# Fourier units spread over two stages, and the modulation steps beside them moved, in a diffusion step's mixing layer

## The chip, the cores and the metric

The kernel runs on one core of a Trainium2 chip. It computes one inference step of one layer for 128 context and 256 latent tokens (384 rows, D = 2048). The metric is device time in microseconds of one launch; the median of three runs stands for a kernel.

## The reference

```python
def mixer(h, s0_f, s0_b, n_chunks, lw):
    proj = h @ lw['w_in']
    q, k, v, g, lr_f, lr_b, fo = jnp.split(proj, splits, axis=-1)
    ...
    o = (o * jax.nn.silu(g.astype(jnp.float32))).astype(h.dtype)     # GLA branch
    fg = fo.astype(jnp.float32).reshape(bsz, t, FOURIER_GROUPS, FOURIER_GROUP_DIM)
    f = jnp.fft.fft2(fg, axes=(1, 3), norm='ortho').real             # Fourier branch
    f = f.reshape(bsz, t, FOURIER_WIDTH).astype(h.dtype)
    gates = jax.nn.sigmoid(h @ lw['w_gate'] + lw['b_gate'])
    g_a, g_b = jnp.split(gates, 2, axis=-1)
    merged = g_a * (o @ lw['w_br_gla']) + g_b * (f @ lw['w_br_four'])
    return merged @ lw['w_out'], s_f, s_b

def layer(x, cond, s0_f, s0_b, n_chunks, lw):
    mod = jax.nn.silu(cond) @ lw['w_ada'] + lw['b_ada']
    sh1, sc1, ga1, sh2, sc2, ga2 = [m[:, None, :] for m in jnp.split(mod, N_MOD, axis=-1)]
    h = rmsnorm(x, lw['norm_pre_mix']) * (1.0 + sc1) + sh1
    m, s_f, s_b = mixer(h, s0_f, s0_b, n_chunks, lw)
    x = x + ga1 * rmsnorm(m, lw['norm_post_mix'])
    h = rmsnorm(x, lw['norm_pre_ffn']) * (1.0 + sc2) + sh2
    ff = (jax.nn.silu(h @ lw['w_ffn_gate']) * (h @ lw['w_ffn_up'])) @ lw['w_ffn_down']
    x = x + ga2 * rmsnorm(ff, lw['norm_post_ffn'])
    return x, s_f, s_b
```

## The kernel before

Activations lie transposed, channels on partitions and the 384 tokens along the rows. Every fp32 product is made of three matmuls on parts in the type fp32r: each weight tile `raw` (128 x 1024, 512 KB) is split into `whi`, a rounded copy made by ScalarE (L218), and `wlo`, the rest, made by VectorE (L219). `gemm` (L252) then multiplies hi by hi, hi by lo and lo by hi.

The weight tiles come in one list `srcs`, in the order in which the products use them. `grab` (L239) hands out the oldest split tile and issues the load and the split of the tile three places further on. `raw` has two buffers, `whi` and `wlo` four each. PE, ScalarE, VectorE and GpSimd keep the order of the program; the order of SP's DMA queue is made by the scheduler when the kernel is built. All DMAs of this part stand in SP's queue.

The stages up to the output projection are: modulation and the first projections; gates and GLA scans (`rate` 1.0); the Fourier projections with the DFT of each group beside them (8 double tiles, `rate` 0.7); the **merge stage**, which the change touches; and the output projection (32 tiles, `rate` 0.6). Beside them a generator `ada_rest` (L555) works out the remaining modulation vectors in steps: 16 full steps per half vector (load 512 KB `adaw`, two VectorE operations on 128 x 1024, L564 and L566), then an empty step, one with 16 small matmuls `pr` (L574), and one with two transposes `ptm`, which also begins the next half. `paced` (L266) takes `rate` steps for each call, so a `rate` of 0.25 is one step in four calls. What is left after output unit 12 is done at once.

The merge stage walks through `mix_order` (L155). It has three kinds of units:

- `o`, 8 of them: one 128-channel tile of GLA's output gate, two weight tiles (48 matmuls `pmm`), then `gcol` (L971): three transposes `pt`, SiLU on ScalarE (with its table), `gs` and `o_lo` on VectorE.
- `b`, 16 of them, `four` (L980): one tile of the Fourier branch's projection, one weight tile, and 34 matmuls `pf` (L990 to L993). Its weight tile is folded first: VectorE makes sums and differences of column pairs (`ws`, L199 and L200) and the split is made of these. Behind PE come two copies on ScalarE and, on VectorE, `fd` (L995), four parts of `y` (L999, L1000) and the product with the gate (L1003). `y` is then written to `four_d` in device memory. If the tile that a `b` unit or an `a` unit prepares is itself a folded one, its split is held until the unit's own work on VectorE is issued (`settle`); in an `o` unit it is made at once.
- `a`, 16 of them: one tile of the GLA branch's projection, one weight tile (24 matmuls), then the product with its gate (L1026), the sum with the `y` of the `b` unit of the same number, read back from `four_d` (L1027, L964), and in the next `a` unit its split into `A_hi` and `A_lo`.

An `a` unit needs all eight `o` units and its own `b` unit. Behind each unit of kind `a` or `b`, `gate_of` (L954) loads the gate (and for `a` the `y`) of the unit two places on and applies the sigmoid to the next one. The order before is o0, o1 b0 b1, o2 b2 b3, ..., o7 b12 b13, then a0 b14 a1 b15, then a2 to a15.

Of the kernel before, what the change touches and what calls it, by code (L numbers as in the profile page):

```python
# [22 lines left out]
KT = D // P  # L23
# [73 lines left out]
def tile_step(ctx: ExitStack, tc: tile.TileContext, a, o):  # L97
# [35 lines left out]
    def alloc_A():  # L133
        return tuple(actp.tile([P, KT, T], F32R, tag=f"A_{n}", name=f"A_{n}") for n in ("hi", "lo"))
# [17 lines left out]
    for i in range(16, 24):  # L152
        srcs += two(a["w_in"], i)

    mix_order = [("o", 0)]  # L155
    for i in range(1, 8):
        mix_order += [("o", i), ("b", 2 * i - 2), ("b", 2 * i - 1)]
    mix_order += [("a", 0), ("b", 14), ("a", 1), ("b", 15)] + [("a", i) for i in range(2, KT)]
    folded = set()
    for b, i in mix_order:  # L160
        if b == "o":
# [66 lines left out]
    def settle():  # L228
        if half_done:
            half_done.pop()()  # L230
# [8 lines left out]
    def grab(hold=False):  # L239
        w = take()  # L240
        push(hold=hold)
        return w

    def step(side):
        if side is not None:
            next(side, None)

    def gemm(dst, w, x, kts, n=P, n0=0, k0=0, first=True, last=True):

        for k in range(kts):  # L250
            for j, (wi, xi) in enumerate(((0, 0), (0, 1), (1, 0))):
                PE.matmul(  # L252
                    dst, w[wi][:, k * n + n0 : k * n + n0 + P], x[xi][:, k0 + k, :],
                    start=first and k == 0 and j == 0, stop=last and k == kts - 1 and j == 2,
                )

    def proj(pool, x, dst, side=None):

        p = pool.tile([P, T], F32, tag="mm", name="pmm")
        for g in range(2):  # L260
            gemm(p, grab(), x, 8, k0=8 * g, first=g == 0, last=g == 1)
            if g:
                dst(p)
            step(side)
# [12 lines left out]
    def split_act(hi, lo, src):  # L277
        ACT.copy(hi, src)
        DVE.tensor_sub(lo, src, hi.bitcast(F32))
# [323 lines left out]
    rate = [1.0]  # L603
# [238 lines left out]
    with ExitStack() as s:  # L842
# [64 lines left out]
        def nyq_weights():  # L907

            n = D // 2
            for h in range(2):  # L910
                wr = pc.tile([P, n], F32, tag="ws", name="wr")
                POOL.memset(wr, 0.0)
                for g in range(4):
                    src = a["w_br_four"][8 * h : 8 * h + 8, 32 * g : 32 * g + 1, (2 * g + 1) * P : (2 * g + 2) * P]
                    SP.dma_start(
                        wr[g : g + 65 : 32, :].rearrange("p (i c) -> p i c", c=P),
                        src.rearrange("i p c -> p i c").to_broadcast([3, 8, P]),
                    )
                    if g % 2:
                        yield  # L920
                w = wn[:, n * h : n * h + n]
                ACT.copy(w, wr)
                DVE.tensor_sub(w[32:64], wr[32:64], w[32:64].bitcast(F32))
                yield
# [8 lines left out]

        sd = side()
        nw = nyq_weights()
        rate[0] = 0.7
        for i in range(8):
            def fo(p, i=i):
                if i % 2 == 0:
# [14 lines left out]
        def gate_of():  # L954

            u = next(gorder, None)
            if u is not None:
                b, i = u
                g = pc.tile([P, T], F32, tag="gate", name="gate", bufs=4)
                SP.dma_start(g, gates_d[i + (16 if b == "b" else 0)])  # L960
                y = None
                if b == "a":
                    y = pc.tile([P, T], F32, tag="yb", name="yb", bufs=4)
                    SP.dma_start(y, four_d[i])  # L964
                gates[u] = g, y
                raw_gates.append(g)
            if raw_gates and (u is None or len(raw_gates) > 1):
                g = raw_gates.pop(0)
                ACT.activation(g, g, AF.Sigmoid)

        def gcol(p, i):  # L971
            pt = pss.tile([P, T], F32, tag="side", name="pt")
            for t in range(3):
                PE.transpose(pt[:, t * P : (t + 1) * P], on(t, i // 2)[:, i % 2, :], ident)
            g = pc.tile([P, T], F32, tag="gs", name="gs")
            ACT.activation(g, p, AF.Silu)
            DVE.scalar_tensor_tensor(g, g, gnorm[:, i : i + 1], pt, op0=ALU.mult, op1=ALU.mult)
            split_act(oT[0][:, i, :], oT[1][:, i, :], g)

        def four(i):  # L980

            w = grab(hold=True)
            d = pc.tile([P, 2, HT], F32, tag="fd", name="fd")
            y = pc.tile([P, T], F32, tag="yb", name="y", bufs=4)
            for m, x in enumerate((eT, dT)):

                pf = (pss if m else psm).tile([P, 512], F32, tag="side" if m else "mm", name="pf")
                for k in range(4):
                    c = slice(512 * m + k * P, 512 * m + (k + 1) * P)
                    PE.matmul(pf[:, 0 : 2 * HT], w[0][:, c], x[k], start=k == 0, stop=False)  # L990
                    PE.matmul(pf[:, 0:HT], w[1][:, c], x[k][:, 0:HT], start=False, stop=m == 1 and k == 3)  # L991
                if m == 0:
                    PE.matmul(pf[:, 0:HT], wn[0:96, i * P : (i + 1) * P], pnr[0:96], start=False, stop=True)  # L993
                ACT.copy(d[:, m], pf[:, HT : 2 * HT])
                DVE.tensor_add(d[:, m], d[:, m], pf[:, 0:HT])  # L995
            g, _ = gates.pop(("b", i))
            for lo, n, base in ((0, TC, 0), (TC, TL, HC)):
                h = n // 2
                DVE.tensor_add(y[:, lo : lo + h], d[:, 0, base : base + h], d[:, 1, base : base + h])  # L999
                DVE.tensor_sub(  # L1000
                    y[:, lo + h : lo + n], d[:, 0, base + h : base : -1], d[:, 1, base + h : base : -1],
                )
            DVE.tensor_mul(y, y, g)  # L1003
            SP.dma_start(four_d[i], y)
            settle()

        rate[0] = 0.25
        mT, late = None, []
        for b, i in mix_order:
            if b == "o":  # L1010
                if i == 1:
                    gate_of()
                proj(psm, hT, lambda p: gcol(p, i), sd)
                if i == 1:
                    gate_of()
                continue
            if b == "b":
                four(i)
            else:
                if mT is None:  # L1020
                    mT = alloc_A()
                    rate[0] = 0.15
                p = psm.tile([P, T], F32, tag="mm", name="pmm")
                gemm(p, grab(hold=True), oT, 8)
                g, y = gates.pop((b, i))
                DVE.tensor_mul(g, g, p)  # L1026
                DVE.tensor_add(y, y, g)  # L1027
                settle()
                if late:
                    split_act(*late.pop())  # L1030
                late.append((mT[0][:, i, :], mT[1][:, i, :], y))
                step(sd)
            gate_of()
# [6 lines left out]
    with ExitStack() as s:  # L1040
# [42 lines left out]
            ACT.activation(sq2, mg32(i), AF.Square)  # L1083
            return sq0, pr, sq2

        rate[0] = 0.6
        spare_h = {-4: ((pe, "hid_hi", 1), (pe, "hid_lo", 1)), -2: ((pe, "S0", 1), (pe, "S1", 1))}
        spare_w = ((adap, "adaw", 2), (adap, "adaw", 2))
        raw2 = None
# [382 lines left out]
        for u in range(HEAD):  # L1472
            kind, c, j = ffn_order[u]
# [316 lines left out]
```

## Time and profile before

| | |
|---|---|
| timed runs, median (lowest, highest) | 1972.66 us (1972.44, 1972.72) |
| profiled execution, first to last instruction (span) | 1970.6 us |
| the rest of a run around such a span | 2.1 us, by the median |
| TensorE matmuls busy | 1949.7 us |
| VectorE busy | 1629.0 us |
| merge stage on PE, o2 to a15 | 603.6 to 767.1 us of the span |

The profiled execution has no time of its own beside its span, so the span is compared with the median. In the profile PE is the matmul part of TensorE, PEld its weight loads, DVE VectorE, ACT ScalarE, POOL GpSimd and SPq SyncE's DMA queue. A row of the timeline gives start and duration in us, engine, line, operation, what is written from what, and in brackets how long the engine had stood idle and what ended that. A matmul's end is modelled and neighbours overlap.

### The profile page before, as it was taken

The numbers are of one execution on the slowest core, as the hardware profiler recorded it, in microseconds if no ns is written. First come the engines' busy times: TensorE is split into PE (matmuls) and PEld (weight loads), VectorE is DVE, ScalarE is ACT, GpSimd is POOL, SyncE is SP. The second block draws the span as 40 slices with busy tenths as digits, with TensorE's granted clock in tenths as the row PEclk, the third lists the DMA queues.
The fourth block names the chain that finished last, engine by engine and source line by source line (L and its number), as shares of the span: only waits on it lengthen the run. The fifth ranks groups of instructions, "written<-read, shape, count | busy, mean of one in ns | idle before, by whom it ended". The sixth has DMA issues, their size and how long they took to land.

```text
span 1970.6 us, 27516 instructions
## 1 busy us (share of the span) xinstructions
PE 1949.7 (99%) x10576; PEld 1727.3 (88%) x10576; DVE 1629.0 (83%) x2075; ACT 908.9 (46%) x1281; POOL 32.2 (2%) x44
## 2 busy tenths in 40 slices
PE   8999999999999999999999999999999999999998
PEld 6779999999999999999988888888888888888886
DVE  5569788878767878877789998999899989887875
ACT  4233554544345655446454444354444444444444
POOL 0000000000000000004000000000000000000001
PEclk9999999999999999999999999999999999999999
DMA  9978677767755687555435444453536363626243
GB/s 389 369 258 271 219 254 238 234 217 247 232 182 180 195 296 233 203 171 180 142 133 183 145 148 156 160 182 123 190 131 201 104 204 109 205 75 192 74 160 130
DMA packets 189411, 380.06 MB, mean 193 GB/s; under 512 B 14172, under 2 KB 112668, under 8 KB 184928
## 3 DMA queue, kind: packets, MB, share of 16 engines
q1 hardware_dynamic: 189136, 377.92, 57.3%
q8 instruction: 83, 1.36, 0.3%
q14 instruction: 48, 0.39, 0.1%
q10 hardware_dynamic: 144, 0.39, 0.1%
HBM read 361.48 MB, written 16.78 MB: 192 GB/s over the span
## 4 chain that ended last, share of the span: by engine, by line
PE 93%; DVE 3%; ACT 2%; DMA 1%; issue 1%; SPq 0%; POOL 0%; DVEq 0%; ACTq 0%; POOLq 0%
PE pmm L252 33%; PE pgu L1492 30%; PE pdn L1492 18%; PE pv L392 3%; PE pgm L375 1%; DMA slab<-in_w_ada 1%; PE px L410 1%; PE pmm L1246 1%; PE ptr L1553 1%; PE pf L990 1%; DVE wlo L219 1%; ACT whi L218 1%; PE po L639 1%; DMA raw<-in_w_d 0%; PE pf L991 0%
## 5 line engine op out<-in xcount | busy, mean ns | idle before, releaser
L252 PE MATMUL pmm<-A_hi,whi 128*128 128x384 f32 x1200 | 404.2, 337 | 0.0
L252 PE MATMUL pmm<-A_hi,wlo 128*128 128x384 f32 x1200 | 401.3, 334 | 0.0
L252 PE MATMUL pmm<-A_lo,whi 128*128 128x384 f32 x1200 | 401.2, 334 | 0.0
L1393 ACT CAST whi<-u 128x1024 fp32r<-128x1024 f32 x200 | 210.6, 1053 | 286.8 <-DVE u L1377 86.2
L1393 ACT CAST whi<-raw 128x1024 fp32r<-128x1024 f32 x175 | 184.3, 1053 | 199.0 <-PE pgu L1492 60.4
L218 ACT CAST whi<-raw 128x1024 fp32r<-128x1024 f32 x181 | 189.9, 1051 | 176.6 <-DMA raw<-in_w_gate 62.4
L1404 DVE TENSOR_TENSOR wlo<-u,whi 128x1024 fp32r<-128x1024 f32 x200 | 243.8, 1219 | 33.0 <-ACT whi L1393 17.8
L219 DVE TENSOR_TENSOR wlo<-raw,whi 128x1024 fp32r<-128x1024 f32 x179 | 217.9, 1221 | 62.1 <-ACT whi L218 61.7
L1492 PE MATMUL pgu<-whi,A_hi 128*128 128x512 f32 x640 | 250.0, 391 | 0.0
L1492 PE MATMUL pgu<-whi,A_lo 128*128 128x512 f32 x640 | 249.3, 389 | 0.0
L1404 DVE TENSOR_TENSOR wlo<-raw,whi 128x1024 fp32r<-128x1024 f32 x175 | 213.2, 1218 | 34.8 <-ACT whi L1393 25.4
L252 PEld LDWEIGHTS pmm<-A_hi,whi 128*128 128x128 f32 x1200 | 225.3, 188 | 2.5 <-issue 1.4
L252 PEld LDWEIGHTS pmm<-A_lo,whi 128*128 128x128 f32 x1200 | 225.4, 188 | 0.2
L252 PEld LDWEIGHTS pmm<-A_hi,wlo 128*128 128x128 f32 x1200 | 225.3, 188 | 0.0
L566 DVE SCALAR_TENSOR_TENSOR adacc<-adaw,spad,adacc 128x1024 f32<-128x1024 f32 x180 | 222.7, 1279 | 0.6 <-DMA adaw<-in_w_ada 0.4
L1492 PE MATMUL pdn<-whi,hid_hi 128*128 128x512 f32 x480 | 186.9, 389 | 0.0
L1492 PE MATMUL pdn<-whi,hid_lo 128*128 128x512 f32 x480 | 186.8, 389 | 0.0
L1492 PE MATMUL pgu<-wlo,A_hi 128*128 128x512 f32 x640 | 184.2, 389 | 0.0
L1492 PEld LDWEIGHTS pgu<-whi,A_hi 128*128 128x128 f32 x640 | 120.1, 188 | 26.1 <-issue 0.8
L1492 PEld LDWEIGHTS pgu<-wlo,A_hi 128*128 128x128 f32 x640 | 120.1, 188 | 25.4
L1492 PEld LDWEIGHTS pgu<-whi,A_lo 128*128 128x128 f32 x640 | 120.2, 188 | 25.1
L1492 PE MATMUL pgu<-whi,S 128*128 128x512 f32 x480 | 131.1, 395 | 0.0
(367 smaller groups left out, 2768.2 us busy)
## 6 DMA issues: line engine op xcount, KB each, us to landing
adaw<-in_w_ada SPq DMA_DIRECT2D x96, 512.0 KB, 4.4
raw<-in_w_d SPq DMA_DIRECT2D x88, 512.0 KB, 3.7
slab<-in_w_ada SPq DMA_DIRECT2D x32, 1024.0 KB
raw<-in_w_gate SPq DMA_DIRECT2D x64, 512.0 KB, 4.6
raw<-in_w_g SPq DMA_DIRECT2D x48, 512.0 KB, 3.2
raw<-in_w_u SPq DMA_DIRECT2D x48, 512.0 KB, 3.4
raw<-in_w_in SPq DMA_DIRECT2D x44, 512.0 KB, 3.5
u<-in_w_u SPq DMA_DIRECT2D x40, 512.0 KB, 4.7
```

The source lines that it names most:

```text
L218: ACT.copy(hi, raw)
L219: sub = lambda: eng.tensor_sub(lo, raw, hi.bitcast(F32))
L252: PE.matmul(dst, w[wi][:, k * n + n0 : k * n + n0 + P], x[xi][:, k0 + k, :], start=first and k == 0 and j == 0, stop=last and k == kts - 1 ...
L375: PE.matmul(pgv[q : q + 32, :], spad[:, k, :], slab[k // (KT // 2)][:, k % (KT // 2), :], start=k < 4, stop=k >= KT - 4,)
L392: PE.matmul(pv[2 * t + g], hT[x_][:, kb, t * P : (t + 1) * P], w_[:, g * 512 : (g + 1) * 512], start=kb == 0 and j == 0, stop=kb == KT - 1 ...
L410: PE.matmul(px, w_[:, u * P : (u + 1) * P], hT[x_][:, kb, :], start=j == 0, stop=j == 2)
L566: DVE.scalar_tensor_tensor(acc[:, c, :], w, spad[:, k, c : c + 1], acc[:, c, :], op0=ALU.mult, op1=ALU.add,)
L639: PE.matmul(dst, w[wi], x[xi], start=first and j == 0, stop=last and j == 2)
L990: PE.matmul(pf[:, 0 : 2 * HT], w[0][:, c], x[k], start=k == 0, stop=False)
L1393: ACT.copy(hi, src)
L1404: DVE.tensor_sub(lo, src, hi.bitcast(F32))
L1492: PE.matmul(dst, stat[x_][m], mov(w[w_], m), start=first and w_ == m == x_ == 0, stop=last and w_ == m == 1,)
```

## The change

`mix_order` is built by other rules. Among the `o` units the `b` units now stand in ones and twos: o0, o1 b0, o2 b1, o3 b2 b3, o4 b4, o5 b5 b6, o6 b7, o7 b8 b9, ten in all. The other six stand singly behind every second `a` unit: a0 b10, a1 a2 b11, a3 a4 b12, up to a9 a10 b15, then a11 to a15. The modulation steps are paced anew: one with each call in the Fourier projections, none in the merge stage, 0.7 with each call in the output projection.

```diff
@@ -152,10 +152,16 @@
-    mix_order = [("o", 0)]
-    for i in range(1, 8):
-        mix_order += [("o", i), ("b", 2 * i - 2), ("b", 2 * i - 1)]
-    mix_order += [("a", 0), ("b", 14), ("a", 1), ("b", 15)] + [("a", i) for i in range(2, KT)]
+    mix_order, n_b = [], 0
+    for i in range(8):
+        k = (0, 1, 1, 2, 1, 2, 1, 2)[i]
+        mix_order += [("o", i)] + [("b", n_b + j) for j in range(k)]
+        n_b += k
+    for i in range(KT):
+        mix_order.append(("a", i))
+        if i % 2 == 0 and n_b < KT:
+            mix_order.append(("b", n_b))
+            n_b += 1
@@ -933,7 +939,7 @@
-        rate[0] = 0.7
+        rate[0] = 1.0
@@ -1004,7 +1010,7 @@
-        rate[0] = 0.25
+        rate[0] = 0.0
@@ -1019,7 +1025,6 @@
-                    rate[0] = 0.15
@@ -1083,7 +1088,7 @@
-        rate[0] = 0.6
+        rate[0] = 0.7
```

From L152 on, lines of the changed kernel have numbers 6 higher (5 higher behind L1022).

VectorE among the `o` units, before, from the end of a unit's second `b`: the product with the gate, the held split, then the next `o` unit.

```order
L1003 TENSOR_TENSOR y<-y,gate 128x384
L219 TENSOR_TENSOR wlo<-ws,whi 128x1024
L199 TENSOR_TENSOR ws<-raw 128x512
L200 TENSOR_TENSOR ws<-raw 128x512
L219 TENSOR_TENSOR wlo<-ws,whi 128x1024
L219 TENSOR_TENSOR wlo<-raw,whi 128x1024
L977 TENSOR_SCALAR gs<-gs,gnorm,pt 128x384
L279 TENSOR_TENSOR o_lo<-gs,o_hi 128x384
L219 TENSOR_TENSOR wlo<-raw,whi 128x1024
L995 TENSOR_TENSOR fd<-fd,pf 128x194 x2
```

The same place of the changed kernel, into o6, which is followed by one `b`:

```order
L1009 TENSOR_TENSOR y<-y,gate 128x384
L225 TENSOR_TENSOR wlo<-ws,whi 128x1024
L225 TENSOR_TENSOR wlo<-raw,whi 128x1024 x2
L983 TENSOR_SCALAR gs<-gs,gnorm,pt 128x384
L285 TENSOR_TENSOR o_lo<-gs,o_hi 128x384
L205 TENSOR_TENSOR ws<-raw 128x512
L206 TENSOR_TENSOR ws<-raw 128x512
L1001 TENSOR_TENSOR fd<-fd,pf 128x194 x2
```

In front of a single `b` the `o` unit prepares two plain tiles; the one fold that used to be done and split at once in the `o` unit is gone from there, and the remaining one stands in the `b` unit, where its split is held.

VectorE among the `a` units, before, behind b15: plain tiles and the three operations of each `a`.

```order
L219 TENSOR_TENSOR wlo<-raw,whi 128x1024
L1026 TENSOR_TENSOR gate<-gate,pmm 128x384
L1027 TENSOR_TENSOR yb<-yb,gate 128x384
L279 TENSOR_TENSOR A_lo<-yb,A_hi 128x384
L219 TENSOR_TENSOR wlo<-raw,whi 128x1024
L1026 TENSOR_TENSOR gate<-gate,pmm 128x384
```

The changed kernel, from the end of b11 to the beginning of b12:

```order
L1009 TENSOR_TENSOR y<-y,gate 128x384
L225 TENSOR_TENSOR wlo<-ws,whi 128x1024
L225 TENSOR_TENSOR wlo<-raw,whi 128x1024
L1031 TENSOR_TENSOR gate<-gate,pmm 128x384
L1032 TENSOR_TENSOR yb<-yb,gate 128x384
L285 TENSOR_TENSOR A_lo<-yb,A_hi 128x384
L225 TENSOR_TENSOR wlo<-raw,whi 128x1024
L1031 TENSOR_TENSOR gate<-gate,pmm 128x384
L1032 TENSOR_TENSOR yb<-yb,gate 128x384
L285 TENSOR_TENSOR A_lo<-yb,A_hi 128x384
L205 TENSOR_TENSOR ws<-raw 128x512
L206 TENSOR_TENSOR ws<-raw 128x512
```

Between two `a` units and the next two there is now the whole VectorE work of a `b` unit.

SP's queue among the `a` units (in brackets the semaphores that an issue waits for: DMAHW of an earlier DMA, DVE, Activation), before:

```order
L190 DMA raw<-in_w_br_gla 128x1024 [waits DMAHW3_49,DVE_49]
L964 DMA yb<-four_d 128x384 [waits DMAHW4_49,DVE_49]
L960 DMA gate<-gates_d 128x384 [waits DMAHW5_49]
L190 DMA raw<-in_w_br_gla 128x1024 [waits DMAHW7_49,DMAHW6_49,DVE_49]
```

The changed kernel, where b11's result is written:

```order
L1010 DMA four_d<-y 128x384 [waits DMAHW0_49,DVE_49]
L966 DMA gate<-gates_d 128x384 [waits Activation_49]
L196 DMA raw<-in_w_br_four 128x1024 [waits DMAHW4_49,DMAHW2_49,DVE_49]
L970 DMA yb<-four_d 128x384 [waits DMAHW3_49,DMAHW0_49]
L966 DMA gate<-gates_d 128x384 [waits DVE_49]
L196 DMA raw<-in_w_br_gla 128x1024 [waits DMAHW6_49,DMAHW5_49,DVE_49]
```

The load of y now follows the write of a `b` unit by three places and waits for a DMA semaphore that, by the turn of the eight, is this write's (DMAHW0); the weight load behind it waits in the queue as well.

## The prediction

> **What bounds the kernel now.** I read the page's busy times first, then what PE waited for.
>
> ```profile
> span 1970.6 us, 27516 instructions
> PE 1949.7 (99%) x10576; PEld 1727.3 (88%) x10576; DVE 1629.0 (83%) x2075; ACT 908.9 (46%) x1281; POOL 32.2 (2%) x44
> PE pf L991 <- DVE wlo L219: 4.7, 5, 1.5
> ```
>
> PE is the bound. Its largest wait in all is in the Fourier units (`pf`): 4.7 us until a weight tile was split. The stretches of this stage, cut where an `o` unit (or `a0`, `a1`, `a2`) starts on PE, show what that costs. Columns: us, then PE, PEld, DVE, ACT and POOL busy, granted clock, DMA share, GB/s.
>
> ```profile
> 603.60:617.10 13.50, 13.50 (x88) 13.46 (x86) 11.26 (x23) 6.73 (x12) 0.00 (x0) 1.00 0.69 218
> 617.10:631.65 14.55, 13.74 (x88) 13.45 (x86) 12.11 (x24) 9.24 (x15) 0.00 (x0) 1.00 0.64 198
> 631.65:646.46 14.81, 13.99 (x88) 13.49 (x86) 12.11 (x24) 9.49 (x15) 0.00 (x0) 1.00 0.62 195
> 646.46:661.26 14.80, 14.80 (x103) 13.89 (x102) 12.10 (x24) 9.49 (x15) 0.00 (x0) 1.00 0.63 197
> 661.26:676.36 15.10, 14.26 (x88) 13.50 (x86) 12.10 (x24) 9.80 (x16) 0.00 (x0) 1.00 0.62 192
> 676.36:691.17 14.81, 13.99 (x90) 13.70 (x88) 12.10 (x24) 9.50 (x15) 0.00 (x0) 1.00 0.62 197
> 691.17:701.79 10.62, 8.32 (x43) 7.74 (x42) 9.19 (x25) 5.41 (x10) 0.00 (x0) 0.88 0.95 353
> 701.79:708.78 6.99, 6.99 (x43) 6.99 (x42) 6.42 (x13) 4.17 (x7) 0.00 (x0) 0.94 0.83 267
> 708.78:767.07 58.29, 58.29 (x339) 58.29 (x338) 46.05 (x70) 28.80 (x48) 0.00 (x0) 1.00 0.86 285
> ```
>
> The first row is one undisturbed group {o,b,b}: 13.5 us. The last is 14 undisturbed `a` units: 58.29 / 14 = 4.16 us each, and an `o`, twice as many such matmuls, 8.33. Between them the same group takes 14.6 to 15.1 us. Why? VectorE's timeline over one group, and two rows of ScalarE:
>
> ```profile
> 613.23 1.23 DVE L219 TENSOR_TENSOR wlo<-ws,whi 128x1024 fp32r<-128x1024 f32 x1 [1.17 <-ACT whi L218]
> 614.37 1.22 DVE L219 TENSOR_TENSOR wlo<-raw,whi 128x1024 fp32r<-128x1024 f32 x1
> 615.98 0.61 DVE L977 SCALAR_TENSOR_TENSOR gs<-gs,gnorm,pt 128x384 f32<-128x384 f32 x1 [0.39 <-ACT gs L976]
> 617.18 0.56 DVE L279 TENSOR_TENSOR o_lo<-gs,o_hi 128x384 fp32r<-128x384 f32 x1 [0.58 <-ACT o_hi L278]
> 619.27 0.61 DVE L995 TENSOR_TENSOR fd<-fd,pf 128x194 f32<-128x194 f32 x2
> 621.20 0.68 DVE L199 TENSOR_TENSOR ws<-raw 128x512 f32<-128x512 f32 x1
> 622.40 0.61 DVE L995 TENSOR_TENSOR fd<-fd,pf 128x194 f32<-128x194 f32 x2
> 624.33 1.22 DVE L219 TENSOR_TENSOR wlo<-ws,whi 128x1024 fp32r<-128x1024 f32 x1
> 625.58 0.69 DVE L199 TENSOR_TENSOR ws<-raw 128x512 f32<-128x512 f32 x1
> 628.04 1.23 DVE L219 TENSOR_TENSOR wlo<-ws,whi 128x1024 fp32r<-128x1024 f32 x1 [1.17 <-ACT whi L218]
> 614.17 1.28 ACT L976 ACT_TABLE_LOAD   x1
> 615.46 0.49 ACT L976 ACTIVATE gs<-pmm 128x384 f32<-128x384 f32 x1
> ```
>
> From 613.23 to 628.04 is 14.81 us, all work or short waits for ScalarE, none for PE. **In {o,b,b} VectorE is slower than PE**, 14.8 against 13.5; PE falls back 1.3 us per group once its lead of split tiles is used up. No modulation step lies in this group: the Fourier units do it.
>
> **The loss.** From 617.10 to 708.78 PE spends 91.7 us. Undisturbed this is five groups, two `a` and two `b` units. Two modulation steps put PE work in there too:
>
> ```profile
> 654.97 0.33 PE pt L974 x3
> 655.30 1.00 PE pr L574 x16
> 488.28 0.22 PE ptm L583 x2
> ```
>
> With `pt`, a `b` is (13.5 − 8.33 − 0.33) / 2 = 2.42 us. So 5 × 13.5 + 2 × 4.16 + 2 × 2.42 = 80.7 us. `pr` and `ptm` are 1.2 us; they cost nothing now (the group with `pr` is as long as its neighbours), but in the Fourier projections, where PE never idles, they are paid. Full gain: 91.7 − 80.7 − 1.2 = **9.8 us**. That is more than PE's idle in the seven disturbed rows (5.6), which starts behind modelled matmul ends and leaves out the stretches at clock 0.88 and 0.94.
>
> On that the Trainium skill, "Perfetto Trace Analysis", section "Identifying the Most-Contended Engine", says that matmul busy time misleads because matmuls are pipelined, and takes weight-load busy time instead. PEld idles 8.9 us in those rows: by PE's idle alone the time would be 1967, by PEld's 1964; the cut by unit starts agrees with the page.
>
> **Fourier units spread.** A group with one `b` costs VectorE, from the pieces above, 1.14 + 1.61 + 1.20 + 0.56 + 1.20 (fold) + 1.93 (fd to y) + 1.25 = 8.9 us against PE's 8.33 + 0.33 + 2.42 = 11.1. It regains 2.2 us in each of the four single groups and loses 1.3 in each of the three double ones, never two in a row. A lead for one double group is there: the first stretch above ran unstalled, the next lost 1.1 of its 1.3. Loss here: 0, at most 0.5.
>
> **The GLA branch's units.** Now a0, b10 and then five times {a,a,b}. An `a` unit, and the ring of two `raw` buffers from load to split:
>
> ```profile
> 626.90 0.33 SPq L190 DMA_DIRECT2D raw<-in_w_in  x1
> 739.56 0.55 DVE L1026 TENSOR_TENSOR gate<-gate,pmm 128x384 f32<-128x384 f32 x1
> 740.62 0.55 DVE L279 TENSOR_TENSOR A_lo<-yb,A_hi 128x384 fp32r<-128x384 f32 x1
> 739.67 0.33 SPq L190 DMA_DIRECT2D raw<-in_w_br_gla  x1
> 744.48 1.05 ACT L218 CAST whi<-raw 128x1024 fp32r<-128x1024 f32 x1 [1.05 <-DMA raw<-in_w_br_gla]
> 745.56 1.23 DVE L219 TENSOR_TENSOR wlo<-raw,whi 128x1024 fp32r<-128x1024 f32 x1 [0.18 <-ACT whi L218]
> raw<-in_w_br_four SPq DMA_DIRECT2D x16, 512.0 KB, 6.2
> ```
>
> VectorE per `a`: 1.14 (`wlo`, as in the group above) + 1.06 + 0.55 = 2.75; per {a,a,b}: 1.20 + 1.93 + 1.25 + 2 × 2.75 = 9.9 us against PE's 2.42 + 2 × 4.16 = 10.7. Tighter, so the ring: a fold frees its buffer 1.32 us after its start (625.58 to 626.90), the next load takes 4.81 until `whi` (739.67 to 744.48), `wlo` follows 1.08 later, then 1.14 and the tail of 1.61 before the next fold: 10.0 us, still under 10.7. With 6.2 us to land it is 11.4.
>
> The lead at the entry: let o7 start on PE at 0. `gs` can start 8.33 + 1.28 + 0.49 + 0.1 = 10.2 us after an `o` starts; with o_lo, fold, y and `wlo` (1.76 + 1.20 + 1.93 + 1.25) VectorE ends a single group at 16.3, so it enters o7 at 16.3 − 11.1 = 5.2, splits two tiles by 10.0, and has b10's tile at 16.3 again. PE reaches b10 at 13.5 + 4.16 = 17.7: 1.4 us of lead. I take 0.3 us for slips here; bounds 0 and 2.
>
> **Modulation steps moved.** By the rates, before: 11 calls in the projections, 6 in the merge stage, and the last (the 109th) in output unit 12. After: 16, 0, and again unit 12. The five that the projections gain are two full steps, one of 1.4 us and two small ones.
>
> ```profile
> 548.00:568.00 20.00, 20.00 (x123) 19.84 (x121) 15.02 (x15) 8.05 (x17) 0.00 (x0) 1.00 0.59 190
> 817.00:842.00 25.00, 25.00 (x146) 25.00 (x146) 22.01 (x26) 10.99 (x18) 0.00 (x0) 1.00 0.64 212
> 811.55 2.48 DVE L566 SCALAR_TENSOR_TENSOR adacc<-adaw,spad,adacc 128x1024 f32<-128x1024 f32 x2
> ```
>
> VectorE is busy 15.0 of 20 us there with three full steps; a fourth makes 17.5. PE's matmuls hide them; without that cover they cost 2 × 2.5 + 1.4 = 6.4 us. Their 512 KB loads pass through SP ahead of weight loads; the DMA share of 0.59 has room. In the output units 17 calls stand where 16 did, closer together; the second row is their busiest stretch now, and VectorE has 3.0 of 25 us left there, room for one more step. I take 0 for both; bounds 0 and 1.
>
> **Sum.** The median of 1972.66 has 2.1 us around the profiled span. 1970.6 − 9.8 + 0.3 = 1961.1 of span, so **1963.2 us**.
>
> **Rivals.**
> (1) *The ring limits {a,a,b}.* For it: a DMA share of 0.86 where only `a` units run. Against it: that stretch also holds two loads of x (L1050). At 6.2 us to land, five groups lose 0.7 each, less the lead of 1.4: 1965. Only with 7.7 us in every group would all the gain be gone: 1972.
> (2) *SP stuck behind Fourier results*, the slower case. The loads of y for `a` units now stand in SP's queue between a Fourier unit's write to `four_d` and later weight loads, and wait for that write.
>
> ```profile
> four_d<-y SPq DMA_DIRECT2D x16, 192.0 KB, 2.9
> 715.49 0.33 SPq L1004 DMA_DIRECT2D four_d<-y  x1
> 722.41 0.80 SPq L964 DMA_DIRECT2D yb<-four_d  x2
> ```
>
> A write lands in 2.9 us, once SP stood until 6.9 behind it. From y's end: 0.2, the write, 0.4, a load of 4.8, 1.1 to the split, whose turn comes a group and 3.2 us after y began, 12.0 after its end. So it binds from 5.5 us of writing on, and must cost 2.8 us in each of five groups (8.3 us writes, every time) to end slower: 1977. The Trainium skill, "DMA: Bandwidth & Descriptors", "Two DMAs through the same engine are not ordered", asks for just such a wait on the first DMA's semaphore; the row of 6.9 us shows one here.
> (3) *Spreading does not help*, the work being the same. Against it: the units from o1 to b15 need 3 × 14.8 + 4 × 8.9 + 5 × 9.9 + 7.1 = 137 us of VectorE and 145 of PE. If VectorE's waits for ScalarE grew as PE's shrank, nothing is won: 1972.
>
> **Chances.** Forecast 0.74; rival 1 0.14, mostly near 1966; rivals 2 and 3 0.06 each. Range 1962.0 (nothing left, and noise) to 1968.0 (the fuller half of rival 1). A measurement can tell about 0.2%, 4 us: faster 0.86, same 0.08, slower 0.06.
>
> **What would show it.** Right: no wait of `pf` for `wlo`, double groups of 13.5 us, single ones of 11.1, {a,a,b} of 10.7, clock 1.00, one more `pr` in the projections. Wrong: `whi` late behind `DMA raw` with PE waiting (rival 1), `yb` rows on SP waiting over 5 us for `four_d` (rival 2), or new PE waits in the projections or the output units.

## The result and the profile after

The changed kernel takes 1964.18 us (median of 4, 1963.93 to 1964.35); beside it the kernel before took 1972.69. The ratio is 0.9957 with a 95% interval of 0.9943 to 0.9971: 8.5 us faster, where 9.5 were forecast (1963.2, range 1962.0 to 1968.0). The page's head, and from the view of waits (us in all, times, longest) what PE still waited for in this stage:

```profile
span 1962.6 us, 27507 instructions
PE 1946.2 (99%) x10576; PEld 1725.5 (88%) x10576; DVE 1629.0 (83%) x2075; ACT 908.0 (46%) x1281; POOL 32.2 (2%) x44
```

```profile
PE pmm L258 <- DVE gate L1031: 0.9, 1, 0.9
PE pf L997 <- DVE wlo L225: 0.2, 1, 0.2
```

VectorE does the same 1629.0 us of work as before, and the 4.7 us of `pf` waiting for a split weight tile have become 0.2. Stretches of the stage follow, cut at unit starts on PE as in the prediction: o4 and o5, the middle one of three pairs of a single and a double group, then a0 b10, a1 a2 b11, the first of the four groups {a,a,b} behind it, and a11 to a15. Columns: us, then PE, PEld, DVE, ACT and POOL busy, granted clock, DMA share, GB/s.

```profile
627.15:638.21 11.06, 11.06 (x70) 11.02 (x69) 9.08 (x21) 7.34 (x10) 0.00 (x0) 1.00 0.70 212
638.21:651.70 13.49, 13.49 (x87) 13.45 (x86) 10.27 (x19) 9.28 (x14) 0.00 (x0) 1.00 0.57 181
...
676.26:682.93 6.67, 6.67 (x44) 6.66 (x42) 5.76 (x13) 4.66 (x7) 0.00 (x0) 1.00 1.00 378
682.93:695.28 12.35, 11.27 (x67) 10.66 (x66) 10.21 (x23) 5.82 (x10) 0.00 (x0) 1.00 0.84 278
695.28:706.01 10.73, 10.73 (x67) 10.73 (x66) 9.94 (x19) 5.56 (x11) 0.00 (x0) 1.00 0.82 262
...
738.26:759.06 20.80, 20.80 (x122) 20.80 (x121) 14.28 (x25) 10.07 (x19) 0.00 (x0) 1.00 0.86 292
```

All three double groups take the undisturbed 13.5 us, where they took up to 15.1; single ones 11.06; the four later groups {a,a,b} 10.73 to 10.76; the clock is 1.00 throughout. One stretch stands out: a1 a2 b11, with 12.35 us, is **1.6 us too long**.

Where did the 8.0 us of span come from? The transposes of o1 are a mark in front of the reordered part, the first matmul of the output stage (767.07 before, 759.06 now) one behind it. The transposes, before and after:

```profile
598.48 0.49 PE L974 MATMUL pt<-ident,qk 128*128 128x128 f32 x3
```

```profile
599.92 0.49 PE L980 MATMUL pt<-ident,qk 128*128 128x128 f32 x3
```

Between the marks PE needed 168.6 us and now needs 159.1: 9.4 us gained. Up to o1 it is 1.4 us later; 1.2 of that are `pr` and `ptm`, which now stand in the projections. Behind the second mark, to the end of the span, both kernels take 1203.5 us. So 9.4 − 1.4 = 8.0, where 11.0 − 0.3 − 1.2 = 9.5 had been forecast.

**The stretch that slips.** SP's queue, ScalarE, VectorE and PE of the changed kernel where a1 follows b10, and that load in the chain of waits (start, us, what):

```profile
674.49 0.86 SPq L1055 DMA_DIRECT2D Chi<-in_xT  x2
685.29 1.05 ACT L224 CAST whi<-raw 128x1024 fp32r<-128x1024 f32 x1 [3.18 <-DMA raw<-in_w_br_gla]
686.37 1.23 DVE L225 TENSOR_TENSOR wlo<-raw,whi 128x1024 fp32r<-128x1024 f32 x1 [1.93 <-ACT whi L224]
688.21 0.41 PE L258 MATMUL pmm<-o_hi,whi 128*128 128x384 f32 x1 [0.92 <-DVE gate L1031]
```

```profile
677.41 7.79 DMA raw<-in_w_br_gla
```

Two loads of x, 768 KB each, are issued 3 us before a GLA tile's weights (677.41). That weight load lands only after 7.8 us. ScalarE waits for it, VectorE's split `wlo` waits for ScalarE, the `gate` product of an `a` unit stands behind the split in VectorE's queue, and PE waits for the buffer of `pmm`, which this product reads.

### The profile page after: what moved, and what is told of

The parts are those of the page before. It is cut to its first block, busy times and chain, and to the rows that moved or that the text cites. A ratio compares the mean times of both kernels' runs of the same rounds, so it can differ in the third digit from the quotient of the medians.

```text
span 1962.6 us, 27507 instructions
## 1 busy us (share of the span) xinstructions
PE 1946.2 (99%) x10576; PEld 1725.5 (88%) x10576; DVE 1629.0 (83%) x2075; ACT 908.0 (46%) x1281; POOL 32.2 (2%) x44
## 4 chain that ended last, share of the span: by engine, by line
PE 95%; DMA 2%; DVE 2%; ACT 1%; issue 0%; SPq 0%; DVEq 0%; ACTq 0%
PE pmm L258 35%; PE pgu L1497 30%; PE pdn L1497 18%; PE pv L398 3%; PE pgm L381 1%; DMA slab<-in_w_ada 1%; PE pf L996 1%; PE px L416 1%; PE pmm L1251 1%; PE ptr L1558 1%; PE po L645 1%; PE pf L997 0%; DMA raw<-in_w_br_gla 0%; DMA raw<-in_w_d 0%; PE pr L580 0%
```

## The experiments

My theory: in {o,b,b} VectorE's work and short waits set the pace; spreading the Fourier units puts each double group beside groups in which VectorE is not late; what is left is the x loads. Rivals: the moved modulation steps are the cause; or ScalarE's chain, the raw ring or the loads set the pace.

### The order alone, the rates alone

The changed kernel with the old rates, and the old order with the new ones:

```diff
-        rate[0] = 1.0
+        rate[0] = 0.7
...
-        rate[0] = 0.0
+        rate[0] = 0.25
...
                     mT = alloc_A()
+                    rate[0] = 0.15
...
-        rate[0] = 0.7
+        rate[0] = 0.6
```

> The changed kernel with the modulation rates of before (0.7, 0.25, 0.15, 0.6). Theory (the order of the Fourier units is the cause): nearly the whole gain stays, 1964 to 1966 us; up to 2 us more than the changed kernel because a modulation step of VectorE (1.4 us) stands again in a GLA-branch group that has only 0.8 us to spare; groups {o,b,b} 13.5 us and {o,b} 11.1 us on TensorE. Rival (the modulation steps moved out of the stage are the cause): 1971 to 1973 us.

> The kernel before with the new modulation rates alone (1.0, 0, 0.7). Theory (order is the cause): groups {o,b,b} stay at 14.8 us; VectorE loses 2 us of modulation work beside a0 and a1, and TensorE pays 1.2 us for pr and ptm in the projections: 1970.5 to 1972.5 us. Rival (the moved modulation steps are the cause): 1964 to 1966 us.

The order alone: 1966.54 us, ratio 0.9971 (0.9961 to 0.9982), 0.5 us above what I had allowed. The rates alone: 1971.63 us, 0.9995 (0.9987 to 1.0004), no difference that can be told. So the order is the cause of most of the gain, 6.1 of 8.5 us. Three stretches of the rates alone, the double group of o5, a0 b14, and a1 b15:

```profile
647.58:662.40 14.82, 14.00 (x87) 13.48 (x86) 12.11 (x24) 9.51 (x15) 0.00 (x0) 1.00 0.61 195
...
692.03:699.95 7.92, 6.90 (x43) 6.45 (x41) 6.38 (x15) 5.62 (x10) 0.00 (x0) 1.00 0.96 361
699.95:707.53 7.58, 6.95 (x43) 6.63 (x42) 7.19 (x17) 3.70 (x7) 0.00 (x0) 1.00 0.86 289
```

The double groups stay at 14.8 us. The entry to the `a` units gets 2.1 us shorter (10.62 + 6.99 before, 7.92 + 7.58 here) and the clock stays at 1.00, but `pr` and `ptm` now cost 1.2 us in the projections. With the new order the rates are worth 2.4 us by the medians, though the two intervals overlap slightly. In the kernel with the order alone, modulation loads stand again in SP's queue, one between the x loads and a GLA tile's (677.22), one 1.1 us ahead of a GLA tile's (718.82). Its stretches a0 b10 and a7 a8 b14 follow.

```profile
677.22 0.33 SPq L567 DMA_DIRECT2D adaw<-in_w_ada  x1
...
718.82 0.33 SPq L567 DMA_DIRECT2D adaw<-in_w_ada  x1
```

```profile
676.13:683.83 7.70, 6.85 (x44) 6.45 (x42) 6.80 (x15) 4.66 (x7) 0.00 (x0) 1.00 0.98 367
...
717.13:729.15 12.02, 11.13 (x68) 10.66 (x66) 10.29 (x19) 5.32 (x10) 0.00 (x0) 1.00 0.79 253
```

a0 b10 is 1.0 us longer than with the new rates (6.67), the group behind it 0.5 shorter (11.83 against 12.35), and the later group 1.3 longer than its undisturbed neighbours (10.74). Another 0.7 us lie behind the stage: from the output projection to the end of the span are 1204.2 us, where before and with the new rates they are 1203.5.

### The x loads held back

`C` is allocated in the loop; VectorE writes one column of each half after a11 and a12, and the loads must wait for that.

```diff
                     mT = alloc_A()
+                    x1, x1t = halves("C")
...
                 DVE.tensor_add(y, y, g)
+                if i in (11, 12):
+                    DVE.tensor_copy(x1t[0][:, 4 * i - 44 : 4 * i - 43, 0:1], y[:, 0:1].unsqueeze(1))
```

> The changed kernel with the two loads of x into the first half of C held back: they wait for a one-column write that VectorE makes after units a11 and a12, and so come 60 us later. Theory (these two loads of 768 KB delay the weight load of the unit behind b10 to 7.8 us, which is the 1.1 us still lost): the wait of pmm for gate goes, span and time 0.8 to 1.3 us shorter, 1962.9 to 1963.4 us. Rival (the tile is late without them too, since VectorE has only 1.4 us of lead there): 1964.2 us, and the wait stays.

> The changed kernel once more, as it is, to stand on one chip beside the next two: 1964 to 1964.5 us.

> The changed kernel with the x loads held back, once more, beside the changed kernel on one chip. Theory: its 1.1 us are real, 1963 to 1963.4 us and no TensorE wait in the stage; rival (the difference was the chip's): equal within 0.3 us.

First time 1963.10 us, 0.9952 (0.9939 to 0.9964). Then both on one chip: the changed kernel 1964.08 (0.9957, 0.9943 to 0.9970), x held back 1963.04 (0.9949, 0.9937 to 0.9962). The intervals overlap, so the time alone does not prove one microsecond, but it came out the same twice and the trace shows where it is. In the first of these runs, a0 b10, a1 a2 b11 and a11 to a15:

```profile
675.92:682.49 6.57, 6.57 (x44) 6.57 (x42) 5.63 (x15) 5.83 (x9) 0.00 (x0) 1.00 0.58 191
682.49:693.23 10.74, 10.74 (x67) 10.74 (x66) 9.70 (x22) 4.78 (x9) 0.00 (x0) 1.00 0.84 274
...
736.22:757.07 20.85, 20.85 (x123) 20.85 (x122) 13.41 (x26) 9.34 (x16) 0.00 (x0) 1.00 0.87 293
```

12.35 has become 10.74, the DMA share beside b10 falls from 1.00 to 0.58, and PE waits nowhere in the stage. The same weight load, issued at 676.63, is split without any wait for it:

```profile
676.63 0.33 SPq L196 DMA_DIRECT2D raw<-in_w_br_gla  x1
...
681.22 1.05 ACT L224 CAST whi<-raw 128x1024 fp32r<-128x1024 f32 x1
```

At most 4.6 us instead of 7.8. From o1's transposes (599.54 here) to the output stage at 757.07 are 157.5 us, 11.1 less than before: the whole gross gain of the prediction, 9.8 + 1.2 = 11.0. This is the lowest time of all the versions, by about 1 us, though the intervals overlap.

### The x loads held back, with the old rates or in the old order

> The new order with the old rates (as in the first experiment, 1966.5 us) and the x loads held back as above. Theory V (the 2.4 us that the old rates cost there are VectorE's modulation work of 2.0 us beside b10 and b11, where it has no slack): at least 1.5 us stay above the new rates with x held, 1964.7 to 1966 us. Rival D (they come from the loads that meet there, 512 KB of modulation weights behind 1.5 MB of x): at most 0.5 us above, under 1964 us.

> The order of before with the new rates and the x loads held back, everything but the new order. Theory (the order gives most, since {o,b,b} stays VectorE's): groups still 14.8 us, and 0 to 1.7 us back beside a0 and a1 where b14 and b15 stand: 1970 to 1971.6 us. Rival (the entry with its loads and modulation steps was the loss, whatever the order): 1967 us or less.

The old order with the new rates and x held: 1971.37 us, 0.9992 (0.9983 to 1.0000). Everything but the order brings 1.7 us by the medians, and the double groups stay:

```profile
647.85:662.66 14.81, 13.99 (x87) 13.48 (x86) 12.11 (x24) 9.50 (x15) 0.00 (x0) 1.00 0.63 196
```

The new order with the old rates and x held: 1967.51 us, 0.9973 (0.9963 to 0.9982), 4.4 above x held with the new rates (the runs spread over 1965.56 to 1969.42; the profiled one took 1966.37). By the total theory V would have it, but the trace doesn't bear that out. Its stretch a0 b10, rows of VectorE and PE at its change to the output stage, then SP's queue and the chain of waits there:

```profile
676.36:683.60 7.24, 6.85 (x44) 6.46 (x42) 6.34 (x14) 5.33 (x8) 0.00 (x0) 1.00 0.69 219
```

```profile
752.56 2.48 DVE L572 SCALAR_TENSOR_TENSOR adacc<-adaw,spad,adacc 128x1024 f32<-128x1024 f32 x2
...
765.07 1.23 DVE L225 TENSOR_TENSOR wlo<-raw,whi 128x1024 fp32r<-128x1024 f32 x1 [2.79 <-ACT whi L224]
...
767.88 0.44 PE L258 MATMUL pmm<-A_lo,whi 128*128 128x384 f32 x1 [1.92 <-DVE A_lo L285]
```

```profile
752.66 0.43 SPq L1058 DMA_DIRECT2D Chi<-in_xT  x1
...
756.57 0.47 SPq L1058 DMA_DIRECT2D Clo<-in_xT  x1
```

```profile
756.20 7.69 DMA raw<-in_w_out
```

Beside b10 the modulation step costs 0.7 us (7.24 against 6.57), and the x loads that meet it there another 0.5 (7.70 without the hold). But here a15's product came behind a late weight split, and PE waited 1.9 us for its result at the start of the output stage, which none of the other kernels shows. So neither theory gave the total. The old rates cost 2.4 us without the hold and 4.4 with it, in several places.

The chain of waits shows how the split became late. VectorE makes a modulation step of 2.48 us (752.56) and only then the split that frees a `raw` buffer, so the next weight load is issued at 756.20. There it meets three loads of x: the two that the hold had sent to this place (752.66 and 753.61), and a third (756.57). It lands after 7.7 us, as the one at the entry did, and the split waits for it. So the hold doesn't remove the meeting of x and weights, it moves it. With the new rates the lead was enough there; with a modulation step in front it was not. Which of the two weighs more isn't shown.

### Less and more work for VectorE

Three versions change only the product of a Fourier result and its gate: on GpSimd and left out (both in the old order), and made twice (in the new order).

```diff
-            DVE.tensor_mul(y, y, g)
+            POOL.tensor_mul(y, y, g)
```

> The kernel before, its order and rates untouched, with the product of a Fourier unit's result and its gate (0.48 us of VectorE) done by GpSimd. Theory (VectorE's work is what makes {o,b,b} slow): a group falls from 14.8 to 13.85 us, so about 0.95 us back in each of five groups and about as much beside a0 and a1: 1966 to 1968 us. Rival (the groups are slow for another reason, the chain through ScalarE or the loads): 1971.5 to 1973 us, groups still at 14.8. A third outcome, VectorE's own instructions becoming longer while GpSimd works, would give 1969 to 1972 with groups between.

> The kernel before without the product of a Fourier unit's result and its gate (that part of the computation is left out): VectorE 0.48 us less per Fourier unit, GpSimd untouched. Theory (VectorE's work sets the length of {o,b,b}): groups of 13.85 us instead of 14.8, so 0.95 us back in each of five groups and 0.5 to 2 beside a0 and a1: 1965.8 to 1967.5 us. Rival (the chain through ScalarE or the loads sets it): 1971.5 to 1973 us.

> The changed kernel with that product made twice (so its result is another): VectorE 0.48 us more per Fourier unit. Theory (with the units spread VectorE has slack in {o,b} and {a,a,b}, which pays for {o,b,b}): VectorE 9.4 us against TensorE 11.1, 15.8 against 13.5, 10.4 against 10.75; over a single and a double group 25.2 against 24.6, so 0.6 us lost three times, and up to 1.4 at the entry to the GLA branch's units as the lead goes: 1965 to 1967.5 us, 1 to 3.3 of the 7.7 us of added work. Rival (VectorE is the bound of the stage in this order too): the whole 7.7 us, 1972 us.

**On GpSimd**: 1974.84 us, 1.0010 (1.0001 to 1.0019), slower, which was in none of my expectations. The timeline of GpSimd and VectorE beside one product, and the double group of o4:

```profile
621.09 0.68 DVE L199 TENSOR_TENSOR ws<-raw 128x512 f32<-128x512 f32 x1
621.32 1.34 POOL L1003 TENSOR_TENSOR y<-y,gate 128x384 f32<-128x384 f32 x1 [9.92 <-DVE y L1000]
621.69 1.51 DVE L200 TENSOR_TENSOR ws<-raw 128x512 f32<-128x512 f32 x1
```

```profile
632.46:647.72 15.26, 14.00 (x87) 13.47 (x86) 12.51 (x22) 9.50 (x15) 3.22 (x2) 1.00 0.60 191
```

The fold that runs beside GpSimd's product takes 1.51 us instead of 0.68: VectorE saves 0.48 and loses 0.83. Its groups become longer, and PE's with them: 15.26 instead of 14.8. That is the third outcome with the other sign, and it speaks for the theory: PE's group length follows VectorE's time upwards too.

**Left out**: 1970.30 us (1967.60 to 1973.45; the profiled run took 1969.28), 0.9987 (0.9979 to 0.9996), a miss by 3 us. Its groups of o3 and o5, the latter with `pr`, then a0 b14 and a1 b15, PE's two waits there, and a piece of the chain of waits in front of them:

```profile
617.01:630.49 13.48, 13.48 (x88) 13.45 (x86) 10.85 (x22) 9.32 (x14) 0.00 (x0) 1.00 0.66 208
...
643.97:658.65 14.68, 14.68 (x104) 13.89 (x102) 11.09 (x22) 9.82 (x16) 0.00 (x0) 1.00 0.65 201
...
686.38:698.04 11.66, 9.19 (x41) 8.61 (x42) 9.47 (x25) 5.61 (x10) 0.00 (x0) 0.79 0.87 329
698.04:705.60 7.56, 7.56 (x44) 7.56 (x42) 6.20 (x13) 5.09 (x9) 0.00 (x0) 0.86 0.83 248
```

```profile
692.41 0.45 PE L990 MATMUL pf<-edT,whi 128*128 128x388 f32 x1 [1.58 <-ACT whi L218]
693.74 0.53 PE L991 MATMUL pf<-edT,wlo 128*128 128x194 f32 x1 [0.89 <-DVE wlo L219]
```

```profile
688.61 1.41 DVE adacc L564 x2
```

The groups did what the theory said and more, down to 13.48 us. Two things I had left out of the expectation: once PE is the bound, `pr` is paid in its group (14.68), and the entry to the `a` units got worse. PE stood 2.5 us there and ran at a granted clock of 0.79 and 0.86 over the two stretches, which is up to 11.66 × 0.21 + 7.56 × 0.14 = 3.5 us (up to, since time spent waiting is in the mean). The chain of waits runs through a modulation step of VectorE in front of b14's fold, 1.9 us with the small operations before the row shown; the missing product does not shorten that.

**Made twice**: 1968.95 us, 0.9980 (0.9971 to 0.9989), 4.8 above the changed kernel where I had allowed 3.3. The groups of o5 and o6:

```profile
638.01:652.35 14.34, 13.75 (x87) 13.45 (x86) 10.37 (x19) 8.41 (x13) 0.00 (x0) 1.00 0.53 172
652.35:664.62 12.27, 11.33 (x70) 11.04 (x69) 10.41 (x23) 7.87 (x13) 0.00 (x0) 1.00 0.65 195
```

A double and a single group together take 14.34 + 12.27 = 26.6 us, 25.2 by my sum. The product, dependent on the one before it, was 0.59 us and not 0.48; three of them in a pair of groups leave 26.6 − 1.8 = 24.8 us, while the changed kernel's pair takes PE 24.55. So in the new order the way through VectorE, its waits included, takes in the `o` part about as long as PE, and the 0.9 us of slack for a pair (24.6 against 14.8 + 8.9) was too much.

### The last six Fourier units singly behind every `a`

```diff
-        if i % 2 == 0 and n_b < KT:
+        if n_b < KT:
```

> The changed kernel with the last six Fourier units singly behind every GLA unit, a0 b10 a1 b11 to a5 b15, instead of behind every second. Theory (a group's VectorE work against its TensorE work decides): VectorE 7.1 us against TensorE 6.6 in {a,b}, so 0.5 us lost in each of six groups less up to 1.4 us of lead: 1965.8 to 1967.5 us. Rival (spacing in this part has no effect): 1964.2 us. Second rival (the ring of two raw buffers decides, each buffer taking 4.8 to 6.2 us to load, 1.1 to the split and 1.2 for it, 7.1 to 8.5 us for 6.6): from 1967 up to 1975 us, with whi waiting for the load just before each lost stretch.

1967.27 us, 0.9973 (0.9963 to 0.9982): the theory's number, but also within the second rival's range. A stretch {a,b} of it, and the split in it:

```profile
699.13:706.43 7.30, 6.86 (x43) 6.54 (x42) 7.00 (x15) 3.69 (x7) 0.00 (x0) 1.00 0.75 254
```

```profile
701.75 1.05 ACT L224 CAST whi<-ws 128x1024 fp32r<-128x1024 f32 x1 [3.62 <-DVE ws L206]
```

VectorE works 7.00 of 7.30 us and PE, which needs 6.6, follows. In each of these groups `whi` waits for VectorE's fold and never for a load, which the second rival had asked for. So with one `a` unit for each `b` VectorE is too slow; with two it is not (10.74 us).

## Why the prediction was right, and where it was off

**The total.** The mechanism was right; the time came nearer than the terms deserved, by luck. The span is 1962.6 us where 1961.1 was the sum: 1.3 us more went at the entry and 0.2 in front of o1. But the 2.1 us put around the span, one run's span set against the median of three, were too many: in the changed kernel's profiled run they are 1.75 (1964.35 against 1962.6), and 1.8 in the runs of the kernel before that have both. So one error hid part of the other.

**VectorE slower than PE in {o,b,b}**: shown from three sides. Order kept, everything else new: 14.8 us. VectorE's work down: 13.48. VectorE's time up: 15.26.

**The loss of 9.8 us net, 11.0 gross**: right. With the x loads held back the stage gains 11.1. Of the old loss up to 10.62 × 0.12 + 6.99 × 0.06 = 1.7 us were clock, by the two rows of before with 0.88 and 0.94. Counting stretches from unit start to unit start took that in; PE's idle alone would not have.

**The `o` part, loss 0**: right in its result, 13.5 and 11.06 us without a wait, but not for its reason. The slack for a pair was taken as 0.9 us, and there is none. Rows of VectorE in the changed kernel, from the fold beside o4 (a single group) to the first beside o5 and to the one beside o6:

```profile
629.54 0.69 DVE L205 TENSOR_TENSOR ws<-raw 128x512 f32<-128x512 f32 x1
...
636.29 1.23 DVE L225 TENSOR_TENSOR wlo<-raw,whi 128x1024 fp32r<-128x1024 f32 x1 [1.26 <-ACT whi L224]
...
639.76 0.68 DVE L205 TENSOR_TENSOR ws<-raw 128x512 f32<-128x512 f32 x1
...
654.58 0.69 DVE L205 TENSOR_TENSOR ws<-raw 128x512 f32<-128x512 f32 x1
```

The double group takes VectorE 14.8 us, as forecast, but the single one 10.2 instead of 8.9: a split waits 1.26 us for ScalarE, which has itself waited 1.87 us for a load. That is 25.0 us for a pair against PE's 24.55. The half microsecond came from the lead of split tiles, and over three pairs the lead was enough.

**{a,a,b}, 10.7 us**: 10.74, and the ring did not limit it.

**The entry, 0.3 us for slips**: the term that was mis-sized; it is 1.6 us, within its own bounds of 0 and 2. I had worked out the lead on VectorE (1.4 us) and not looked at what lands in SP's queue at that moment. The x loads were in front of me, in the argument on rival 1, and a loading time of 7.7 us too; there I asked whether it holds in every group, not whether it happens once. It happened once, and holding those loads back removes it.

**The modulation steps**: the way up to o1 became 1.4 us longer where 1.2 were put for `pr` and `ptm`; the output stage lost nothing, as forecast. What the forecast didn't say is that the steps, left in the merge stage, would cost the new order 2.4 us: the rates are no bystander but a part of the gain. In the old order the 1.0 us by the medians can't be told from nothing.

**Rivals.** The ring did not limit the groups {a,a,b}. Its sign, `whi` late behind a load with PE waiting, came once, at the entry. That SP stands behind Fourier results is so, and PE waited for none of it. SP's queue of the changed kernel (us in all, times, longest), and the place of the longest wait:

```profile
SPq L970 <- DMA four_d<-y: 12.4, 6, 4.1
```

```profile
744.45 0.33 SPq L1010 DMA_DIRECT2D four_d<-y  x1
...
750.91 0.80 SPq L970 DMA_DIRECT2D yb<-four_d  x2
```

The limit was 5.5 us from the write to the load of y. Behind b10 to b14 these are 3.8 to 4.8 us. Behind b15 they are 6.5, more than the limit, but no Fourier group follows there (before, the 6.9 us of the prediction stood at the same unit). That spreading doesn't help: refuted.

## What to carry to other kernels

Where two engines alternate as the bound, add up each engine's time for every group of the repeating order, waits on third engines included, and mix the groups so that none of them stays over the other's time for long; the total of busy time says nothing about it. When PE stops waiting, work that was hidden in its waits (`pr` here) must be paid, and small neighbours (a modulation step, a load of x) become the next bound, so move them in the same change. A large load that nobody needs soon should not stand in front of a weight load at a place where the lead is thin: here that was worth the last 1 us. Look too at where the held load goes: it can meet other weights there.

## What the runs showed of the hardware

- A 512 KB load landed after 7.8 us when issued 3 us behind two loads of 768 KB, and within 4.6 us without them. Another landed after 7.7 us with loads of x issued 3.5 and 2.6 us before it and 0.4 us behind it.
- GpSimd's product of two SBUF tiles beside VectorE's difference of two SBUF tiles: the difference took 1.51 us instead of 0.68. The Trainium skill, "SBUF — State Buffer", section "SBUF: two separate sides", calls the port pair that the two share an exclusive lock, the loser blocking fully; the 0.83 us agree with a block and not with a small slowdown.
- The granted clock fell after short waits that came in pairs: 0.82 and 1.48 us around one matmul in the kernel before, 1.58 and 0.89 without the product (0.90 and then 0.67 in two stretches of 4 us before, 0.66 and 0.50 without the product). It did not fall after a single wait of 1.92 us (1.00 in the microseconds behind it, with the old rates and x held). The Trainium skill, "TensorE: Matmul & The Clock Gate", section "What's actually happening", puts the fall after an idle window of about 3.4 us; here 2.3 to 2.5 us of waiting within 3 us did it. What decides between these cases these runs don't show.
